# Rotary embedding in a decoder trunk: exchanging halves by ScalarE copies instead of permutation matmuls

## The chip, the cores and the metric

One core of one Trainium2 chip runs the kernel. The metric is the device time of one execution in microseconds (us), the median over several runs. TensorE multiplies matrices (PE in the profile, its weight loads PEld), VectorE is DVE, ScalarE is ACT, GpSimd is POOL, and SyncE (SP) issues most loads.

## What is computed

The reference is a trunk of two identical layers over 512 tokens of width 1024. A layer normalises x, projects it with one wide matrix, runs four causal mixers on the parts (forgetting attention "fox", gated linear attention "gla", retention "ret", and the state-space mixer "ssd"), gates and sums them, and adds a SwiGLU block. The change touches the rotary embedding of the retention mixer alone: q and k, four heads of 64 each, have their two halves of 32 turned against each other.

```
def apply_rotary(x, cos, sin):
    x1, x2 = xf[..., :half], xf[..., half:]        # half = 32 of a head's 64
    return concatenate([x1 * cos - x2 * sin, x1 * sin + x2 * cos])

o_c = retention_chunked(apply_rotary(heads(rq), cos, sin),
                        apply_rotary(heads(rk), cos, sin), heads(rv), log_gamma)
```

So an output element is its own value times cosine, plus or minus the value 32 rows away times sine.

## The kernel before, in words

Activations lie transposed: features on the 128 partitions, the 512 tokens along the row. A tile of q or k of the retention mixer is 128 x 512 and holds two heads, so the exchange of halves is an exchange between neighbouring groups of 32 partitions. There are two such tiles of q (`rq`) and two of k (`rk`) per layer.

Matrices are multiplied in float32r, a rounded float32, in two or three passes: an operand is split into a rounded part and a difference (`split`, line 211: a copy on ACT, a subtraction on DVE), and `mm3` (line 200) makes three matmuls of them, `mm2` (line 206) two, where one operand is an exact constant.

Weights come in pieces of eight 128 x 128 blocks. `load` (line 245) issues one transfer on SP into one of two buffers, and `convert` (line 257) splits it, so each piece costs one ACT cast (L212) and one DVE subtraction (L213) of 128 x 1024. The pool of pieces has three buffers of each kind (line 139). The order of the blocks is that in which the program asks for them.

A projection (`proj`, line 435) is 8 blocks times three matmuls of 512 columns into one PSUM bank of the pool `pm`, which has four (line 144). `scaled` (line 484) takes it out of the bank with one DVE product (L487 or L489) into a tile from the pool `tp`, which has 33 tiles of 128 x 512 (lines 174 and 176). Mixers' own products go into four other banks, the pool `px` (line 145).

The order of work is written by hand. Each mixer is a generator that yields between steps. `drain` (line 462) runs one and, at each yield, lets `pull` (line 455) take projections, gates and up-projections from the list `fill`, until their stated costs reach the yield's weight times the mixer's entry in `PACE` (line 41). The list is filled at lines 1182 to 1195. The projections of `rq` and `rk` are the last four of the twelve that are listed before `ssd()`, and so are pulled towards the end of that mixer (lines 1184 and 1185). After that come `gla()`, `ret()` and `fox()`. The program is then given to a planner with a simulated timeline (line 1503), which lays out the order on each engine and assigns the tiles' places.

`ret` (line 914) begins with the rotary embedding: `split_tile` of the four tiles (line 916), a yield of weight 0.8, the multiplication of each by the constant signed permutation `perm` (line 920), a yield, then for each tile the product of the permuted tile with `sinT` on DVE (line 925), the product of the tile itself with `cosT` on POOL (line 926), the sum on DVE (line 927), and a yield. Seven more yields follow in the rest of the mixer. `sinT` and `cosT` are made once per launch by `rotary` (line 352). The constants that must be exact are loaded and cast at the start by `constants` (line 313); `perm` is 128 of their 780 columns.

The lines that the diff leaves as they are but that its steps go through:

```
def drain(gen, us):
    for want in gen:
        pull(us * (1 if want is None else want))
...
fill += [keep(rq, j, C_RQ + P * j) for j in range(2)] + [keep(rk, j, C_RK + P * j) for j in range(2)]
drain(ssd(), PACE[0])
...
drain(gla(), PACE[1])
...
drain(ret(), PACE[2])
```

Of the kernel before, what the change touches and what calls it, by code (L numbers as in the profile page):

```python
# [13 lines left out]
AF = mybir.ActivationFunctionType  # L14
# [4 lines left out]
P = 128  # L19
# [18 lines left out]
WARM = 11  # L38
TILE = 5.2
LAG = 1  # L40
PACE = (4.5, 5.0, 5.0, 7.5)
WIDE = 256 + 28
PARTS = (6, 6, 6, 4)
PLAIN = 2
# [11 lines left out]
def _const_parts():  # L56
    i = np.arange(P)
    same = (i[:, None] // 64) == (i[None, :] // 64)
    up = (i[:, None] <= i[None, :]).astype(np.float64)
    perm = np.zeros((P, P))  # L60
    for m in range(P):
        if m % 64 < 32:
            perm[m + 32, m] = -1.0
        else:
            perm[m - 32, m] = 1.0
    dret = np.zeros((P, NH, P))
    rel = i[None, :] - i[:, None]
    for h in range(NH):
        dret[:, h, :] = np.where(rel >= 0, np.exp(np.maximum(rel, 0) * LOGG[h]), 0.0) * 0.125
    qdec = np.zeros((P, 2, P))  # L70
    for j in range(2):
        for half in range(2):
            qdec[64 * half:64 * half + 64, j, :] = np.exp((i + 1.0) * LOGG[2 * j + half])[None, :]
    kdec = np.exp((P - 1.0 - i)[:, None] * LOGG[None, :]) * 0.125
    inv = (10000.0 ** (-np.arange(32) / 32.0))[i % 32][:, None]
    sgn = np.repeat(np.array([-1.0] * 4 + [1.0] * 8)[None, :], P, 0)
    one = np.ones((P, 1))
    exact = [
        ("uo", np.concatenate([up, np.ones((P, P))], 1)),
        ("lst", (i[:, None] > i[None, :]).astype(np.float64)),  # L80
        ("bones", same.astype(np.float64)),
        ("ubd", up * same),
        ("perm", perm),
        ("sel8", ((i[:, None] % 8 == np.arange(8)[None]) & (i[:, None] < 64)).astype(np.float64)),
        ("sel4", ((i[:, None] % 4 == np.arange(4)[None]) & (i[:, None] % 32 < 16) & (i[:, None] < 64)).astype(np.float64)),
    ]
    return exact, [
        ("ident", np.eye(P)),
        ("dret", dret.reshape(P, -1)),
        ("qdec", qdec.reshape(P, -1)),  # L90
        ("kdec", kdec),
        ("inv", inv),
        ("sgn", sgn),
        ("blk8", (i[:, None] // 8 == np.arange(4)[None]).astype(np.float64)),
        ("blk4", (i[:, None] // 4 == np.arange(4)[None]).astype(np.float64)),
        ("eps", one * EPS),
        ("one", one),
        ("hpi", one * (math.pi / 2)),
    ]
# [33 lines left out]
def trunk(ctx: ExitStack, tc: tile.TileContext, keys, qkeys, xin, pos, wst, wsq, par, ext, cst, out):  # L133
# [200 lines left out]
    def R(n):  # L334
        o, w = EXACT_OFF[n]
        return cr[:, o:o + w]

    ident = C("ident")
    lst, bones, ubd, perm, uo = (R(n) for n in ("lst", "bones", "ubd", "perm", "uo"))
    sel8 = R("sel8").rearrange("p (g r) -> p r g", g=2)  # L340
    sel4 = R("sel4")
    U, ones = uo[:, :P], uo[:, P:2 * P]
# [9 lines left out]
    def rotary():  # L352
        ang = TT()
        V.tensor_copy(out=ang, in_=posi.pop())
        V.tensor_scalar(out=ang, in0=ang, scalar1=C("inv"), scalar2=None, op0=ALU.mult)
        n = TT()
        V.tensor_scalar(out=n, in0=ang, scalar1=1.0 / (2 * math.pi), scalar2=12582912.0, op0=ALU.mult, op1=ALU.add)
        V.tensor_scalar(out=n, in0=n, scalar1=-12582912.0, scalar2=None, op0=ALU.add)
        for c in _two_pi_parts():
            V.scalar_tensor_tensor(out=ang, in0=n, scalar=-c, in1=ang, op0=ALU.mult, op1=ALU.add)  # L360
        V.tensor_scalar(out=ang, in0=ang, scalar1=3.1415925, scalar2=-3.1415925, op0=ALU.min, op1=ALU.max)
        act(out=sinT, in_=ang, func=AF.Sin)
        act(out=n, in_=ang, func=AF.Abs)
        act(out=cosT, in_=n, func=AF.Sin, scale=-1.0, bias=hpi)

# [69 lines left out]
    def proj(name, l, c, src, nk):  # L435
        ps = MM()
        for k in range(nk):
            mm3(ps, block(name, l, k, c), src[k], k == 0, k == nk - 1)
        return ps

    def layer(l, n1, scope):
# [67 lines left out]
        def keep(dst, i, c, scale=None):  # L509
            def go():  # L510
                dst[i] = scaled(proj("w_in", l, c, n1, KD), scale)
            return TILE, go

        def tokmajor(dst, c, stacked=False):
# [397 lines left out]
        yc = [None] * 2  # L912

        def ret():
            pp = []
            sr = [split_tile(t) for t in rq + rk]
            yield 0.8
            for t in sr:
                ps = MX()
                mm2(ps, perm, t, True, True)  # L920
                pp.append(ps)
            yield
            for ps, t in zip(pp, rq + rk):
                u = TT()
                V.tensor_tensor(out=u, in0=ps, in1=sinT, op=ALU.mult)
                G.tensor_tensor(out=t, in0=t, in1=cosT, op=ALU.mult)
                V.tensor_tensor(out=t, in0=t, in1=u, op=ALU.add)
            yield
            qd = []
            for j in range(2):  # L930
                t = TT()
                G.tensor_tensor(out=chunked(t), in0=chunked(rq[j]), in1=qdec[:, j].unsqueeze(1).broadcast_to([P, NB, P]), op=ALU.mult)
                qd.append(t)
            ms = {}
            for j in range(2):
                pa = [MX(), MX()]
                for tb in range(NB):
                    ts = slice(tb * P, (tb + 1) * P)
                    for half in range(2):
                        hs = slice(64 * half, 64 * half + 64)  # L940
                        mm(pa[half][:, ts], rk[j][hs, ts], rq[j][hs, ts], True, True)
                for half, ps in enumerate(pa):
                    t = TT()
                    V.tensor_tensor(out=chunked(t), in0=chunked(ps), in1=dret[:, 2 * j + half].unsqueeze(1).broadcast_to([P, NB, P]), op=ALU.mult)
                    ms[j, half] = t
                yield
            kt = []
            for j in range(2):
                ps = MX()
                for tb in range(NB):  # L950
                    T.transpose(ps[:, tb * P:(tb + 1) * P], rk[j][:, tb * P:(tb + 1) * P], ident)
                t = TT()
                V.tensor_tensor(out=t.rearrange("p (c h n) -> p c h n", c=NB, h=2), in0=ps.rearrange("p (c h n) -> p c h n", c=NB, h=2), in1=kdec[:, 2 * j:2 * j + 2].unsqueeze(1).unsqueeze(3).broadcast_to([P, NB, 2, 64]), op=ALU.mult)
                kt.append(t)
            yield
            ps = MX()
            pv = ps[:, :384].rearrange("p (c j n) -> p c j n", c=3, j=2)
            for c in range(3):
                for j in range(2):
                    for half in range(2):  # L960
                        hd = 2 * j + half
                        mm(pv[64 * half:64 * half + 64, c, j], kt[j][:, c * P + 64 * half:c * P + 64 * half + 64], rv[0][:, c, hd * 64:(hd + 1) * 64], True, True)
            for c in range(3):
                for half in range(2):
                    hs = slice(64 * half, 64 * half + 64)
                    if c == 0:
                        V.tensor_copy(out=sbd[hs, 0, :, hs], in_=pv[hs, 0])
                    else:
                        for j in range(2):
                            V.scalar_tensor_tensor(out=sbd[hs, c, j, hs], in0=sbd[hs, c - 1, j, hs], scalar=float(np.exp(P * LOGG[2 * j + half])), in1=pv[hs, c, j], op0=ALU.mult, op1=ALU.add)  # L970
            yield
            pos_ = [MX(), MX()]
            for j, po in enumerate(pos_):
                for c in range(NB):
                    ts = slice(c * P, (c + 1) * P)
                    for half in range(2):
                        hd = 2 * j + half
                        mm(po[64 * half:64 * half + 64, ts], rv[0][:, c, hd * 64:(hd + 1) * 64], ms[j, half][:, ts], c == 0, False)
            for j, po in enumerate(pos_):
                for c in range(1, NB):  # L980
                    ts = slice(c * P, (c + 1) * P)
                    mm(po[:, ts], sbd[:, c - 1, j], qd[j][:, ts], False, c == NB - 1)
            yield
            yield from headnorm(pos_, PR("rn"), gates["r"][2:], yc)
# [196 lines left out]

        fill += [keep(gq, j, C_GQ + P * j, 0.125) for j in range(2)] + [keep(gk, j, C_GK + P * j) for j in range(2)]
        fill += silus([C_GR, C_GR + P, C_RG, C_RG + P])
        fill += [keep(rq, j, C_RQ + P * j) for j in range(2)] + [keep(rk, j, C_RK + P * j) for j in range(2)]
        drain(ssd(), PACE[0])
        fill += tokmajor(rv, C_RV)
        fill += gate_quad(3, 0) + mix(gate_quad(3, 1), up_of(3, 0))
# [341 lines left out]
```

## Time and profile before

| | us |
|---|---|
| median of 3 runs | 1717.92 |
| lowest and highest | 1717.42, 1718.14 |
| profiled execution, its own time | 1718.72 |
| span of that execution in the profile | 1717.0 |

The profile shows one execution. Its span runs from the first to the last instruction of the program; 1.72 us of the execution's own time lie around it. Times of rows are microseconds from the span's start. A line such as L198 is a line of the kernel; where a helper records the instruction (`mm`, `split`, `act`), the line is the helper's, and the tile names tell which step it is. In a tile pair such as `mx<-t,cr` the left side is what is written (`mx` is a bank of the mixers, `mm` one of the projections), the right side what is read (`t` is a tile of the pool `tp`, `cr` the exact constants, `cs` the others, `xh` and `xl` the split activations, `wh` and `wl` the split weights).

### The profile page before, as it was taken

What the parts mean: (1) busy time and instruction counts of PE and PEld (TensorE: products, weight loads), DVE (VectorE), ACT (ScalarE), POOL (GpSimd) and SP (SyncE); (2) the same over time, 40 slices, a digit from 0 to 9 for tenths busy, and PEclk for the clock granted to TensorE, in tenths of its full rate; (3) what the DMA queues carried; (4) which work ended last, traced back from release to release, by engine and by line L of the source; (5) the groups of instructions that cost most, each with busy time, mean ns of one, the idle gap of its engine ahead of it and who ended that gap; (6) DMA issues with size and microseconds to landing.
All of it is one profiled execution on the core that took longest, in us unless ns stands there. A gap on an engine that the chain in (4) does not pass through costs nothing.

```text
span 1717.0 us, 25146 instructions
## 1 busy us (share of the span) xinstructions
PE 1705.9 (99%) x10140; PEld 1484.7 (86%) x10140; DVE 1213.2 (71%) x1683; ACT 861.9 (50%) x1190; POOL 225.2 (13%) x227
## 2 busy tenths in 40 slices
PE   8999999999999999999999999999999999999998
PEld 7878888888888999998988788888888889999998
DVE  5867666768677677675777666767776677767666
ACT  5424543546447646464544254435553574655543
POOL 2032110022101010101010322200221010101010
PEclk9999999999999999999999999999999999999999
DMA  5322222222235657575333222222222365665653
GB/s 199 106 74 74 75 82 78 86 86 74 78 112 143 196 134 186 135 186 121 89 99 115 68 74 75 85 76 89 83 86 82 103 172 161 152 175 139 183 108 102
DMA packets 54693, 195.00 MB, mean 114 GB/s; under 512 B 6064, under 2 KB 6448, under 8 KB 54576
## 3 DMA queue, kind: packets, MB, share of 16 engines
q1 hardware_dynamic: 45072, 160.45, 29.2%
q0 software_dynamic: 8640, 31.46, 10.3%
q8 instruction: 79, 1.29, 0.3%
q10 hardware_dynamic: 864, 1.48, 0.2%
q14 instruction: 38, 0.31, 0.1%
HBM read 191.27 MB, written 2.10 MB: 113 GB/s over the span
## 4 chain that ended last, share of the span: by engine, by line
PE 97%; DVE 1%; DMA 1%; ACT 1%; issue 0%; ACTq 0%; DVEq 0%
PE mm L198 65%; PE mx L198 31%; PE mx L1079 0%; DMA x<-in_x_dram 0%; DMA t<-in_ext_dram 0%; ACT wh L212 0%; DVE wl L213 0%; PE mx L679 0%; DVE t L369 0%; ACT L231 0%; DVE t L836 0%; ACT g L236 0%; DVE t L1168 0%; DVE n L407 0%; PE mx L871 0%
## 5 line engine op out<-in xcount | busy, mean ns | idle before, releaser
L212 ACT CAST wh<-wr 128x1024 fp32r<-128x1024 f32 (+1 forms) x240 | 250.0, 1043 | 378.4 <-PE mm L198 238.0
L198 PE MATMUL mm<-xh,wh 128*128 128x512 f32 (+1 forms) x1184 | 429.2, 362 | 0.9 <-DVE t L1168 0.9
L198 PE MATMUL mm<-xh,wl 128*128 128x512 f32 (+1 forms) x1184 | 428.6, 362 | 0.0
L198 PE MATMUL mm<-xl,wh 128*128 128x512 f32 (+1 forms) x1184 | 427.4, 361 | 0.0
L213 DVE TENSOR_TENSOR wl<-wr,wh 128x1024 fp32r<-128x1024 f32 (+1 forms) x220 | 281.8, 1282 | 119.9 <-ACT wh L212 117.6
L198 PEld LDWEIGHTS mm<-xh,wh 128*128 128x128 f32 x1184 | 222.6, 188 | 35.2 <-DVE t L1168 1.8
L198 PEld LDWEIGHTS mm<-xh,wl 128*128 128x128 f32 x1184 | 222.6, 188 | 35.1 <-issue 1.5
L198 PEld LDWEIGHTS mm<-xl,wh 128*128 128x128 f32 x1184 | 222.6, 188 | 33.7 <-issue 1.1
L198 PE MATMUL mm<-t,wh 128*128 128x512 f32 x448 | 140.3, 392 | 0.0
L198 PE MATMUL mx<-xh,wh 128*128 128x256 f32 (+1 forms) x448 | 136.2, 311 | 3.0 <-ACT wh L212 3.0
L198 PE MATMUL mx<-xl,wh 128*128 128x256 f32 (+1 forms) x448 | 138.5, 309 | 0.0
L1287 POOL DMA_DIRECT2D wl<-in_wsq_dram x60 | 51.9, 864 | 518.0 <-ACT wl L1286 337.1
L198 PE MATMUL mx<-f,wh 128*128 128x512 f32 x352 | 108.3, 390 | 0.0
L198 PE MATMUL mm<-f,wh 128*128 128x512 f32 x352 | 106.0, 390 | 0.0
L198 PEld LDWEIGHTS mm<-t,wh 128*128 128x128 f32 x448 | 83.3, 188 | 17.1
L213 DVE TENSOR_TENSOR l<-rq,wh 128x1024 fp32r<-128x1024 f32 x60 | 73.2, 1219 | 33.1 <-ACT wh L212 18.7
L198 PEld LDWEIGHTS mx<-xh,wh 128*128 128x128 f32 x448 | 84.1, 188 | 9.2 <-ACT wh L212 4.0
L198 PE MATMUL mx<-xh,wl 128*128 128x256 f32 (+1 forms) x288 | 91.0, 327 | 0.0
L198 PEld LDWEIGHTS mx<-xl,wh 128*128 128x128 f32 x448 | 84.2, 188 | 5.1
L198 PE MATMUL mm<-t,wl 128*128 128x512 f32 x224 | 87.5, 390 | 0.0
L212 ACT CAST wh<-rq 128x1024 fp32r<-128x1024 f32 x60 | 62.9, 1049 | 43.9 <-PE mm L198 21.5
L198 PEld LDWEIGHTS mm<-f,wh 128*128 128x128 f32 x352 | 66.1, 188 | 13.5
(275 smaller groups left out, 3457.2 us busy)
## 6 DMA issues: line engine op xcount, KB each, us to landing
wr<-in_wst_dram SPq DMA_DIRECT2D x216, 512.0 KB, 3.5
rq<-in_wsq_dram SPq DMA_DIRECT2D x60, 512.0 KB, 5.3
wl<-in_wsq_dram POOLq DMA_DIRECT2D x60, 512.0 KB, 7.1
wr<-in_wsq_dram SPq DMA_DIRECT2D x20, 512.0 KB, 7.3
out_dram<-x SPq DMA_DIRECT2D x8, 256.0 KB, 2.0
x<-in_x_dram SPq DMA_DIRECT2D x3, 512.0 KB, 7.2
wr<-in_wst_dram SPq DMA_DIRECT2D x4, 256.0 KB, 5.6
x<-in_x_dram SPq DMA_DIRECT2D x2, 256.0 KB, 4.5
```

The costliest lines, as they stand in the source:

```text
L198: T.matmul(o, lhsT=l, rhs=r, start=start, stop=stop, skip_group_check=True)
L212: A.copy(out=hi, in_=src)
L213: V.tensor_tensor(out=lo, in0=src, in1=hi.bitcast(F32), op=ALU.subtract)
L1287: G.dma_start(out=lo, in_=wsq[j], accum_op=ALU.add)
```

## The change

The permutation matmuls, their splits and the constant go. In place of `keep`, the four tiles of `rq` and `rk` get a new entry of the list, `turned`, which does the whole rotary embedding right behind the evacuation of the projection: four ACT copies of 32 partitions each write the tile with its halves exchanged into a second tile, and then the two products and the sum are made as before, the product with `sinT` now reading that second tile where it read a PSUM bank. The sign of the permutation moves into `sinT`, as a scale of its one activation by a constant column `turn`. The three yields of the removed part go, and the pace of `ret` rises from 5.0 to 7.0.

```diff
-PACE = (4.5, 5.0, 5.0, 7.5)
+PACE = (4.5, 5.0, 7.0, 7.5)
...
-        ("perm", perm),
...
+        ("turn", np.where(i % 64 < 32, -1.0, 1.0)[:, None]),
...
-        act(out=sinT, in_=ang, func=AF.Sin)
+        act(out=sinT, in_=ang, func=AF.Sin, scale=C("turn"))
...
+        def turned(dst, i, c):
+            def go():
+                t = dst[i] = scaled(proj("w_in", l, c, n1, KD))
+                u = TT()
+                for a in range(0, P, 32):
+                    A.copy(out=u[a:a + 32], in_=t[a ^ 32:(a ^ 32) + 32])
+                V.tensor_tensor(out=u, in0=u, in1=sinT, op=ALU.mult)
+                G.tensor_tensor(out=t, in0=t, in1=cosT, op=ALU.mult)
+                V.tensor_tensor(out=t, in0=t, in1=u, op=ALU.add)
             return TILE, go
...
         def ret():
-            pp = []
-            sr = [split_tile(t) for t in rq + rk]
-            yield 0.8
-            for t in sr:
-                ps = MX()
-                mm2(ps, perm, t, True, True)
-                pp.append(ps)
-            yield
-            for ps, t in zip(pp, rq + rk):
-                u = TT()
-                V.tensor_tensor(out=u, in0=ps, in1=sinT, op=ALU.mult)
-                G.tensor_tensor(out=t, in0=t, in1=cosT, op=ALU.mult)
-                V.tensor_tensor(out=t, in0=t, in1=u, op=ALU.add)
-            yield
             qd = []
...
-        fill += [keep(rq, j, C_RQ + P * j) for j in range(2)] + [keep(rk, j, C_RK + P * j) for j in range(2)]
+        fill += [turned(rq, j, C_RQ + P * j) for j in range(2)] + [turned(rk, j, C_RK + P * j) for j in range(2)]
```

## Rows read from the trace of the kernel before

**Rows 1.** The page's first part, busy time of each engine with its share of the span and its instructions, and from its second part the granted clock of TensorE in 40 slices, in tenths of full speed.
```profile
PE 1705.9 (99%) x10140; PEld 1484.7 (86%) x10140; DVE 1213.2 (71%) x1683; ACT 861.9 (50%) x1190; POOL 225.2 (13%) x227
PEclk9999999999999999999999999999999999999999
```
**Rows 2.** All waits of PE over the whole span: who waited for whom, us in total, times, longest.
```profile
PE mx L198 <- ACT wh L212: 3.0, 3, 1.6
PE mm L198 <- POOL t L325: 1.4, 1, 1.4
PE mx L198 <- DVE t L213: 1.2, 2, 0.7
PE mm L198 <- DVE t L1168: 0.9, 2, 0.5
```
**Rows 3.** PE's timeline in layer 0: start, duration, engine, line, operation, tiles, shapes. Between the first two rows lie 27 more matmuls of projections, between the third and the fourth 18 more, six of them of the permutation (one row of the view can hold two).
```profile
244.72 0.39 PE L198 MATMUL mm<-xh,wh 128*128 128x512 f32 x1
...
251.07 0.40 PE L198 MATMUL mm<-xl,wh 128*128 128x512 f32 x1
251.30 0.40 PE L198 MATMUL mx<-t,cr 128*128 128x512 f32 x1
...
255.70 0.40 PE L198 MATMUL mx<-t,cr 128*128 128x512 f32 x1
255.94 0.39 PE L198 MATMUL mm<-xh,wl 128*128 128x512 f32 x1
```
**Rows 4.** PE's groups by line and shape: the group of all matmuls of 512 columns that read an exact constant, with their count, busy time, mean ns of one and idle time before them.
```profile
L198 PE MATMUL mx<-t,cr 128*128 128x512 f32 x96 | 35.0, 401 | 0.0
```
**Rows 5.** Two lines of the kernel by themselves: a cast of 32 partitions that stays in place (L610), and one of 64 partitions from one half to the other (L1045). Columns: count, duration in ns (min/median/max), first and last start, forms.
```profile
L610 ACT CAST t<-t x4: 618/620/622, 100.4 to 1143.4; 32x512 fp32r<-32x512 f32 x4
...
L1045 ACT CAST t<-t x8: 617/618/620, 341.8 to 1264.8; 64x512 fp32r<-64x512 f32 x8
```
**Rows 6.** The timeline of layer 0 at the retention mixer's split (L916, recorded at the lines of `split`): three ACT casts in a row, one DVE difference alone and three in a row, the idle time before them and who ended it in brackets.
```profile
247.62 1.66 ACT L212 CAST t<-t 128x512 fp32r<-128x512 f32 x3
...
246.79 0.69 DVE L213 TENSOR_TENSOR t<-t,t 128x512 fp32r<-128x512 f32 x1 [3.19 <-ACT t L212]
...
249.87 2.98 DVE L213 TENSOR_TENSOR t<-t,t 128x512 fp32r<-128x512 f32 x3
```
**Rows 7.** DVE's timeline in layer 0: evacuations of projections (L487). Where the idle time before one was ended by PE, it took the bank as soon as PE had filled it.
```profile
135.01 0.68 DVE L487 TENSOR_TENSOR t<-mm,n 128x512 f32<-128x512 f32 x1
...
146.77 1.28 DVE L487 TENSOR_TENSOR t<-mm,n 128x512 f32<-128x512 f32 x2
...
152.05 0.69 DVE L487 TENSOR_TENSOR t<-mm,n 128x512 f32<-128x512 f32 x1 [2.42 <-PE mm L198]
...
165.25 0.69 DVE L487 TENSOR_TENSOR t<-mm,n 128x512 f32<-128x512 f32 x1 [0.33 <-PE mm L198]
```
**Rows 8.** Busy time of each engine in three stretches of layer 0 (start:end, length, then PE, PEld, DVE, ACT and POOL with their instructions, granted clock, DMA share, GB/s).
```profile
146.00:166.00 20.00, 20.00 (x135) 15.98 (x134) 14.12 (x21) 13.32 (x20) 5.54 (x5) 1.00 0.23 78
166.00:186.00 20.00, 20.00 (x144) 18.74 (x143) 14.85 (x20) 13.21 (x25) 2.27 (x5) 1.00 0.25 79
...
247.00:262.00 15.00, 15.00 (x67) 12.38 (x66) 14.63 (x17) 4.38 (x6) 9.48 (x6) 1.00 0.19 70
```
**Rows 9.** The list of waits over all engines: ACT's weight casts.
```profile
ACT wh L212 <- PE mm L198: 259.5, 98, 7.5
```
**Rows 10.** Timelines of layer 0: the last differences of the split of the state-space mixer's result on DVE, and the first up-projection on PE, which reads that result.
```profile
174.68 1.29 DVE L213 TENSOR_TENSOR t<-t,t 128x512 fp32r<-128x512 f32 x2
...
216.44 0.71 PE L198 MATMUL mm<-t,wh 128*128 128x512 f32 x2
```
**Rows 11.** The three elementwise lines of the rotary embedding, with the columns of rows 5.
```profile
L925 DVE TENSOR_TENSOR t<-mx,sinT x8: 673/678/680, 255.0 to 1109.6; 128x512 f32<-128x512 f32 x8
...
L926 POOL TENSOR_TENSOR t<-t,cosT x8: 1293/1702/2284, 247.6 to 1104.8; 128x512 f32<-128x512 f32 x8
...
L927 DVE TENSOR_TENSOR t<-t,t x8: 679/862/999, 255.8 to 1111.6; 128x512 f32<-128x512 f32 x8
```
**Rows 12.** The start of the launch: the second transfer of the exact constants among the DMA issues (queue, count, KB, us to landing), three pieces of the chain that ended last (start, us, what), and one stretch of the busy times with the columns of rows 8.
```profile
t<-in_ext_dram ACTq DMA_DIRECT2D x1, 134.0 KB, 5.5
...
1.74 5.54 DMA t<-in_ext_dram
...
7.30 7.24 DMA x<-in_x_dram
...
20.52 4.64 PE mx L198 x19
...
5.00:10.00 5.00, 3.42 (x18) 2.81 (x18) 2.64 (x4) 4.96 (x8) 1.02 (x2) 1.00 1.03 394
```
**Rows 13.** PE's timeline in layer 0 around the retention mixer's scores: 32 small full-precision matmuls between projections.
```profile
262.74 0.39 PE L198 MATMUL mm<-xh,wl 128*128 128x512 f32 x1
263.06 2.06 PE L198 MATMUL mx<-t,t 64*128 64x128 f32 x32
265.04 0.50 PE L198 MATMUL mm<-xh,wh 128*128 128x512 f32 x1
265.38 0.39 PE L198 MATMUL mm<-xl,wh 128*128 128x512 f32 x1
```

More of the change, by code (lines that the diff above doesn't have):

```diff
@@ L59, in _const_parts @@
     up = (i[:, None] <= i[None, :]).astype(np.float64)
[L60 to L65, printed above, removed]
     dret = np.zeros((P, NH, P))
@@ L338, in trunk @@
     ident = C("ident")
-    lst, bones, ubd, perm, uo = (R(n) for n in ("lst", "bones", "ubd", "perm", "uo"))
+    lst, bones, ubd, uo = (R(n) for n in ("lst", "bones", "ubd", "uo"))
     sel8 = R("sel8").rearrange("p (g r) -> p r g", g=2)
@@ L511, in go @@
                 dst[i] = scaled(proj("w_in", l, c, n1, KD), scale)
+            return TILE, go
+        def turned(dst, i, c):
[7 more added lines that the diff above has]
+                V.tensor_tensor(out=t, in0=t, in1=u, op=ALU.add)
             return TILE, go
```

## Prediction

> **What bounds the kernel now.** I read the page's engine line first: TensorE (PE) is busy for 99% of the span, VectorE (DVE) 71%, ScalarE (ACT) 50%, GpSimd (POOL) 13%, and the granted clock is 9 tenths or more in every slice [rows 1]. Next the list of waits, for PE alone: 6.5 us in the whole span, 4.4 of them PE on ACT and POOL, and the other four waits, 2.1 us together, on DVE [rows 2]. So PE is the bound, and what is worth something is what PE's own stream loses.
>
> The busy time of a matmul is no price, since each overlaps the next; the distance between starts is. In a stretch without permutations PE makes 28 matmuls of 512 columns from 244.72 to 251.07, which is 6.35 / 28 = 0.2268 us each, and the rows read 0.39 us for the same thing [rows 3]. The even spacing shows that the 99% is real.
>
> **What PE loses.** In each layer the permutation is four products of two matmuls (L920), so eight of 512 columns, sixteen in all; they are among the 96 matmuls that read an exact constant with 512 columns [rows 4]. Between the starts at 251.07 and 255.94 PE runs 21 matmuls, these eight and 13 of a projection woven between them [rows 3]. It takes 4.87 us; 13 at 0.2268 are 2.95; the eight cost 1.92, 0.240 each. The weaving also shows that nobody waits for the permutation: the planner (line 1503) lays projections around it, and PE doesn't idle there. So its whole worth is its own time: 16 x 0.240 = 3.84 us. The lower bound is the plain spacing, 16 x 0.2268 = 3.63.
>
> The Trainium skill (TensorE: Matmul & The Clock Gate, "Wait — 56ns, not 53.3ns?") gives 215.7 ns between starts for 512 columns at the full clock; by that figure the term would be an estimated 3.45 us. The trace's own spacing is longer, and I use it.
>
> **What the split loses.** L916 makes a rounded copy on ACT (three take 1.66 us in a row; with 0.62 for the last one [rows 5] they are 0.52 apart) and a difference on DVE (0.69 alone, 2.98 for three beside POOL), four of each per layer [rows 6]. Per layer ACT loses 2.2 us and DVE 2.8 to 4.0. PE waits for neither there; worth 0, as nothing on the path is late by it.
>
> **What the copies add.** Each of the four tiles of a layer gets four copies of 32 partitions by 512. No row shows a copy between 32-partition groups. The nearest are a 32 x 512 cast that stays in place, 0.62 us, and a 64 x 512 cast from one half of the partitions to the other, 0.618 [rows 5]: fewer partitions are no cheaper, and crossing costs nothing. So 16 copies a layer take 16 x 0.52 = 8.3 us back to back, or 9.9 at the whole duration. I take 8.3, since the four follow each other on one tile. They come behind the evacuations of these projections (L487), the last four of which in layer 0 start between 146.77 and 165.25 [rows 7]. ACT is busy 13.32 us in 146 to 166 and 13.21 in 166 to 186, of 20 each [rows 8]: 26.5 + 8.3 = 34.8 of 40, with the upper price 36.4. They fit, but if all sixteen fell into the first 20 us they would need 21.6.
>
> What is queued behind them on ACT? First, weight casts (L212): these start when PE frees a piece, as 259.5 us of ACT's idle time ended so [rows 9]; there are three pieces (line 139), each worth 8 blocks of three matmuls, 24 x 0.2268 = 5.4 us of PE. Four copies ahead delay a cast by about 2.2 us, which the piece in hand covers. Second, the squares and norm of the SSD mixer, whose result PE first needs at 216.44, the first up-projection, while the last differences of its split on DVE end near 176 [rows 10]. Forty microseconds cover a delay of two to nine.
>
> **What moves.** The product with sinT (0.678 us, the same each time), the product with cosT on POOL (1.29 to 2.28) and the sum (0.68 to 1.00) keep their number [rows 11], and go from the retention stage to the SSD tail. The product with sinT will read two SBUF tiles in place of a PSUM bank and one; the nearest row of that kind is the sum, so 0.68 to 1.00. That adds at most 0.32 x 4 = 1.3 us per layer to DVE, which has 14.12 of 20 us busy there, while the stretch it leaves, 247 to 262, is almost full on DVE with 14.63 of 15 [rows 8]. The Trainium skill speaks against the move (SBUF — State Buffer, "Who interferes with whom"): a DVE instruction with two SBUF inputs and a POOL instruction that reads SBUF shut each other out for a whole instruction, so each product could wait for one cosT product. By that rule an estimated 8 x 1.29 us more waiting on DVE or POOL, none of it on PE. The constant 0.678 beside the spread of the sum agrees with the rule.
>
> DVE now waits for ACT's copies in its own queue, and behind it stand the evacuations of the next projections and the weight differences. This is priced as a rival below; as the forecast I take 0.
>
> **The pace.** The three yields that go were worth 0.8 + 1 + 1 of ten; 9.8 yields at 5.0 pull 49 us of projections into the retention stage, 7 at 7.0 pull 49. Equal, 0. The sign enters as a scale of the one sine activation that the whole launch makes, and its constant is one column: 0.
>
> **The head.** The table of exact constants is 128 columns narrower, 64 KB. The chain of waits begins with the second transfer of that table (134 KB, now 70), 5.54 us from 1.74; the load of x at 7.30 goes out only when it has landed, takes 7.24, and PE's unbroken run starts at 20.52 [rows 12]. From 5 to 10 us the engines move 394 GB/s [rows 12]; 64 KB is 0.16 us at that rate. Bounds: 0, if the next load is limited by the other traffic, and 0.5, three times its bytes, if the landing and the load behind it both move. I take 0.16.
>
> **Sum.** 3.84 + 0.16 = 4.00. The profiled execution took 1718.72 us, 1.72 over its span of 1717.0, and 0.80 above the median of 1717.92. So 1718.72 - 4.00 = 1714.72 by that execution, and 1713.9 as a median. With the bounds, 3.63 to 4.34: 1714.3 to 1713.6. A measurement of this kernel can tell about 0.2%, 3.44 us; the border is 1714.48, close above the forecast.
>
> **Rivals.**
> Order given back (1715.9). The planner lays out each engine's order, and one edit changes it elsewhere. Every visit of PE to small full-precision matmuls among the projections costs about 0.2 us: 0.32 from 262.74 to 263.06 in place of 0.227, and 0.34 from 265.04 to 265.38 [rows 13]. Ten more visits over two layers cost 2.0. For it: the SSD tail, where the work lands, is full of such visits. Against: as likely to be fewer.
>
> More gained (1711.8). PE waits four times on DVE, twice each for L1168 and L213 (0.9 + 1.2) [rows 2]; if DVE, relieved in the retention stage, runs ahead, these waits vanish: 2.1 more. Against: the work before them is much the same.
>
> Slower (1725). The working tiles come from a pool of 33 (line 174), and now each turned projection takes a second one. In the SSD stage evacuations already lag: none between 135.01 and 146.77, then two at once, while those at 152.05 and 165.25 wait for PE [rows 7]. So at 146.77 two of the four projection banks (line 144) are full and a third is filling. If every turned tile held the next back by its copies, POOL product and sum, 2.2 + 1.3 + 0.9 = 4.4 us, four make 17.6 per layer, against the 12 us or so by which an evacuation was late without a stall (135.01 to 146.77). PE would stall 5.6 us a layer, 11.2 in all: 1713.9 + 11.2. It decides from about 14 us of lag per layer; that is where the gain of 2 us a layer is gone. Against: the lag is over by 152, as the SSD's tiles are set free.
>
> Nothing comes off (1717.9): the planner leaves PE idle where the permutations were. Only if the retention stage had nothing else ready; 49 us of projections speak against it.
>
> **How the numbers follow.** Forecast 0.50, more gained 0.10, order given back 0.30, nothing 0.03, slower 0.07. Faster by over 0.2%: 0.50 + 0.10 = 0.60; within: 0.33; slower: 0.07. The range leaves out the slower case, nothing, and the outer half of more gained, and so goes from 1711.4 to 1717.2.
>
> **What would show it.** Right: 16 fewer matmuls that read exact constants with 512 columns (80), plain spacing unchanged at 0.227, PE's waits near 6.5 us, ACT over 16 us busy in the 20 us around the rotated projections, sixteen copies per layer near 0.62 us, the sinT product spreading up to 1.00. Wrong: new PE waits on DVE or ACT between 140 and 190, or in the same place of layer 1; a first up-projection later than 216 by more than a few microseconds; copies of over 1 us.

## The result, and the profile after

The changed kernel takes 1726.01 us (median of 6 runs, 1724.58 to 1726.90) against 1718.22 for the kernel before on the same chip (6 runs): a ratio of 1.0045, 95% interval 1.0035 to 1.0054. It is slower by 7.8 us. The prediction was 1713.9, with 1711.4 to 1717.2 as its range.

The profiled execution took 1726.06 us, with a span of 1724.3 where before it was 1717.0. From here on, lines of the changed kernel are those of its own file: `mm` is L192 (before L198), `split` L206 and L207 (L212 and L213), the up-projections' evacuation L1159 (L1168). The page's engine line, answering [rows 1]:

```profile
PE 1708.8 (99%) x10124; PEld 1485.1 (86%) x10124; DVE 1199.4 (70%) x1675; ACT 875.2 (51%) x1214; POOL 225.3 (13%) x227
```

PE makes 16 matmuls fewer and is busy 2.9 us longer. The 40 slices of the granted clock are all at 9 tenths or more, as before, and too coarse to show why. All waits of PE, answering [rows 2]:

```profile
PE mm L192 <- DVE t L1159: 6.7, 2, 3.3
PE mx L192 <- ACT wh L206: 2.7, 3, 1.2
PE mm L192 <- POOL t L319: 1.4, 1, 1.4
```

The first row is the one to read: the wait for the up-projections' evacuation, 0.45 us a layer before, is 3.34 us a layer now. PE's timeline at the two places, both at the start of the forgetting attention, some 75 us behind the place that the permutation matmuls had:

```profile
331.02 0.40 PE L192 MATMUL mx<-t,cr 128*128 128x512 f32 x1
334.76 0.80 PE L192 MATMUL mm<-xh,wh 128*128 128x512 f32 x1 [3.34 <-DVE t L1159]
335.35 0.63 PE L192 MATMUL mm<-xl,wh 128*128 128x512 f32 x1
335.78 0.63 PE L192 MATMUL mm<-xh,wl 128*128 128x512 f32 x1
...
337.86 0.40 PE L192 MATMUL mm<-xl,wh 128*128 128x512 f32 x1
...
1188.70 0.79 PE L192 MATMUL mm<-xh,wh 128*128 128x512 f32 x1 [3.34 <-DVE t L1159]
...
1194.41 0.45 PE L192 MATMUL mm<-xl,wh 128*128 128x512 f32 x1
```

Two losses stand here. The wait itself: 331.02 to 334.76 is 3.74 us for a step of 0.23. And what follows it: 335.35 to 335.78 is 0.43 us a matmul where it was 0.227 [rows 3]. Seven matmuls from 334.76 to 337.86 take 3.10 us, 1.5 more than at 0.227; in layer 1, 13 from 1188.70 to 1194.41 take 5.71, 2.8 more. The granted clock says so too, in the busy times of these stretches (start:end, length, then PE, PEld, DVE, ACT and POOL with their instructions, granted clock, DMA share, GB/s):

```profile
322.00:330.00 8.00, 8.00 (x36) 6.53 (x36) 4.99 (x7) 6.18 (x10) 0.00 (x0) 1.00 0.20 67
330.00:338.00 8.00, 4.66 (x15) 3.47 (x14) 7.53 (x12) 6.14 (x6) 0.00 (x0) 0.79 0.24 69
1184.00:1196.00 12.00, 8.66 (x26) 6.54 (x26) 11.52 (x18) 7.72 (x9) 0.00 (x0) 0.72 0.14 44
```

In 330 to 338 PE is busy for 4.66 of 8 us at a granted clock of 0.79; in the 8 us ahead of that the clock is 1.00. The matmuls at 0.43 us are at the lower of its two levels, 1.2 GHz.

Why the evacuation is late is on DVE, in the same stretch:

```profile
325.53 0.69 DVE L1159 TENSOR_TENSOR t<-mm,g 128x512 f32<-128x512 f32 x1
326.13 1.28 DVE L362 SCALAR_TENSOR_TENSOR t<-mx,t 128x512 f32<-128x512 f32 x2
328.95 0.69 DVE L362 SCALAR_TENSOR_TENSOR t<-mx,t 128x512 f32<-128x512 f32 x1 [1.55 <-ACT t L230]
330.47 1.23 DVE L207 TENSOR_TENSOR wl<-wr,wh 128x1024 fp32r<-128x1024 f32 x1 [0.83 <-ACT wh L206]
331.62 1.29 DVE L363 SCALAR_TENSOR_TENSOR t<-t,t 128x512 f32<-128x512 f32 x2
332.82 0.69 DVE L362 SCALAR_TENSOR_TENSOR t<-mx,t 128x512 f32<-128x512 f32 x1
333.42 0.69 DVE L363 SCALAR_TENSOR_TENSOR t<-t,t 128x512 f32<-128x512 f32 x1
334.02 1.28 DVE L1159 TENSOR_TENSOR t<-mm,g 128x512 f32<-128x512 f32 x2
```

L362 to L364 are the Newton steps of the forgetting attention's norm of q and k: a chain that waits for ACT's exponentials. One evacuation stands ahead of it, two behind eight more instructions, seven of the chain and a weight difference (L207). The same stretch of the kernel before, DVE (L368 to L370 are its Newton steps, L1168 the evacuation) and PE:

```profile
328.53 1.28 DVE L369 SCALAR_TENSOR_TENSOR t<-t,t 128x512 f32<-128x512 f32 x2
329.73 0.68 DVE L368 SCALAR_TENSOR_TENSOR t<-mx,t 128x512 f32<-128x512 f32 x1
330.33 1.28 DVE L1168 TENSOR_TENSOR t<-mm,g 128x512 f32<-128x512 f32 x2
```
```profile
330.22 0.40 PE L198 MATMUL mx<-t,cr 128*128 128x512 f32 x1
331.06 0.50 PE L198 MATMUL mm<-xh,wh 128*128 128x512 f32 x1 [0.45 <-DVE t L1168]
```

The two evacuations started at 330.33, behind six instructions of the chain (the weight difference was done ahead of it, at 323.24), and PE took the bank 0.45 us late. Now they start at 334.02, 3.7 us later, though PE comes to the place only 0.8 us later (331.02 against 330.22). Nothing in this stretch belongs to the rotary embedding. What differs is the order that the planner laid out.

The rest of what the change did: PE's group that answers [rows 4], the transfer that answers [rows 12], copies, sinT product and sum (columns of [rows 11]), and the two stretches of [rows 8].

```profile
L192 PE MATMUL mx<-t,cr 128*128 128x512 f32 x80 | 28.7, 402 | 0.0
```
```profile
t<-in_ext_dram ACTq DMA_DIRECT2D x1, 70.0 KB, 5.5
```
```profile
L513 ACT COPY t<-t x32: 614/617/622, 152.4 to 1025.3; 32x512 f32<-32x512 f32 x32
...
L514 DVE TENSOR_TENSOR t<-t,sinT x8: 691/692/1787, 155.0 to 1026.0; 128x512 f32<-128x512 f32 x8
...
L516 DVE TENSOR_TENSOR t<-t,t x8: 679/693/1782, 158.9 to 1028.0; 128x512 f32<-128x512 f32 x8
```
```profile
146.00:166.00 20.00, 20.00 (x137) 16.04 (x137) 15.44 (x19) 15.51 (x23) 9.49 (x6) 1.00 0.21 55
166.00:186.00 20.00, 20.00 (x133) 18.30 (x132) 16.91 (x24) 14.33 (x25) 4.12 (x3) 1.00 0.26 78
```

The matmuls are gone, the copies cost what the 32 x 512 cast cost [rows 5], and in the last two rows, the place where they now stand, PE is busy for 20.00 of 20 us at the full clock.

**The sum of 7.3 us of span.** Removed matmuls: -3.8. The wait, 6.7 in place of 0.9: +5.8. The clock: 1.5 and 2.8, +4.3. That is 6.3. Of the remaining 1.0, I can place +1.2 (matmuls of up to 128 columns in layer 0 take 44.4 us by the distance of their starts, where it was 43.2: the retention scores among them 1.6 more, of which more under "The second price", while a wait of 0.5 on L213 is gone) and -1.1 (a stretch near the end in which this one execution of before ran slower, shown at the third experiment); 0.9 stays unplaced.

### The profile page after: what moved, and what is told of

Its sections match the earlier page's. It is cut to its first block, busy times and chain, and to the rows that moved or that the text cites. A ratio compares the mean times of both kernels' runs of the same rounds, so it can differ in the third digit from the quotient of the medians.

```text
span 1724.3 us, 25119 instructions
## 1 busy us (share of the span) xinstructions
PE 1708.8 (99%) x10124; PEld 1485.1 (86%) x10124; DVE 1199.4 (70%) x1675; ACT 875.2 (51%) x1214; POOL 225.3 (13%) x227
## 4 chain that ended last, share of the span: by engine, by line
PE 97%; DVE 1%; DMA 1%; ACT 0%; issue 0%; SPq 0%; DVEq 0%
PE mm L192 66%; PE mx L192 31%; PE mx L1070 1%; DMA x<-in_x_dram 0%; DMA wr<-in_wst_dram 0%; DVE t L363 0%; PE mx L684 0%; DVE wl L207 0%; ACT wh L206 0%; DVE t L841 0%; PE mx L942 0%; PE mx L876 0%; DVE n L401 0%; DVE t L847 0%; DVE t L1159 0%
## 5 line engine op out<-in xcount | busy, mean ns | idle before, releaser
L206 ACT CAST wh<-wr 128x1024 fp32r<-128x1024 f32 (+1 forms) x240 | 250.0, 1043 | 393.8 <-PE mm L192 239.1
L192 PE MATMUL mm<-xh,wh 128*128 128x512 f32 (+1 forms) x1184 | 430.4, 363 | 6.7 <-DVE t L1159 6.7
L192 PE MATMUL mm<-xh,wl 128*128 128x512 f32 (+1 forms) x1184 | 429.9, 363 | 0.0
L192 PE MATMUL mm<-xl,wh 128*128 128x512 f32 (+1 forms) x1184 | 429.4, 363 | 0.0
L207 DVE TENSOR_TENSOR wl<-wr,wh 128x1024 fp32r<-128x1024 f32 (+1 forms) x220 | 275.5, 1254 | 141.7 <-ACT wh L206 139.1
L192 PEld LDWEIGHTS mm<-xh,wh 128*128 128x128 f32 x1184 | 223.5, 189 | 41.0 <-DVE t L1159 7.5
L192 PEld LDWEIGHTS mm<-xl,wh 128*128 128x128 f32 x1184 | 223.5, 189 | 34.9 <-issue 1.6
L192 PEld LDWEIGHTS mm<-xh,wl 128*128 128x128 f32 x1184 | 223.5, 189 | 34.4 <-issue 0.9
L192 PE MATMUL mm<-t,wh 128*128 128x512 f32 x448 | 140.7, 393 | 0.0
L192 PE MATMUL mx<-xh,wh 128*128 128x256 f32 (+1 forms) x448 | 135.9, 310 | 2.7 <-ACT wh L206 2.7
L192 PE MATMUL mx<-xl,wh 128*128 128x256 f32 (+1 forms) x448 | 138.3, 309 | 0.0
L192 PE MATMUL mx<-f,wh 128*128 128x512 f32 x352 | 108.2, 390 | 0.0
L192 PE MATMUL mm<-f,wh 128*128 128x512 f32 x352 | 105.9, 389 | 0.0
L192 PEld LDWEIGHTS mm<-t,wh 128*128 128x128 f32 x448 | 83.4, 188 | 17.3
L207 DVE TENSOR_TENSOR l<-rq,wh 128x1024 fp32r<-128x1024 f32 x60 | 73.2, 1221 | 32.7 <-ACT wh L206 18.6
L192 PEld LDWEIGHTS mx<-xh,wh 128*128 128x128 f32 x448 | 84.1, 188 | 8.8 <-ACT wh L206 3.8
L192 PE MATMUL mx<-xh,wl 128*128 128x256 f32 (+1 forms) x288 | 90.9, 327 | 0.0
L192 PEld LDWEIGHTS mx<-xl,wh 128*128 128x128 f32 x448 | 84.1, 188 | 5.1
L192 PE MATMUL mm<-t,wl 128*128 128x512 f32 x224 | 87.5, 391 | 0.0
L206 ACT CAST wh<-rq 128x1024 fp32r<-128x1024 f32 x60 | 63.0, 1050 | 43.7 <-PE mm L192 17.9
L192 PEld LDWEIGHTS mm<-f,wh 128*128 128x128 f32 x352 | 66.1, 188 | 13.5
```

The source lines that it names most:

```text
L192: T.matmul(o, lhsT=l, rhs=r, start=start, stop=stop, skip_group_check=True)
L206: A.copy(out=hi, in_=src)
L207: V.tensor_tensor(out=lo, in0=src, in1=hi.bitcast(F32), op=ALU.subtract)
```

## The experiments

Theory 1: not the copies but the edit of pace and yields costs, by where it puts the up-projections' evacuations. Theory 2: the rotary work in the state-space tail makes ACT and DVE late. Theory 3: the permutation matmuls were not worth 3.8 us.

**e1: the kernel after, with pace and yields undone.**

```diff
-PACE = (4.5, 5.0, 7.0, 7.5)
+PACE = (4.5, 5.0, 5.0, 7.5)
...
         def ret():
+            yield 0.8
+            yield
+            yield
             qd = []
```

> The kernel after with one part undone: the pace of the retention mixer back to 5.0 and its three yields (0.8, 1, 1) back at its start; the copies, the new place of the products and the missing permutation matmuls stay. Theory 1 (the edit of pace and yields moved the norm chain of the forgetting attention ahead of the up-projections' evacuations): no wait of PE over 1 us on L1159's evacuations, no fall of the granted clock, 1714 us (1713 to 1716). Theory 2 (the copies and products in the state-space tail make DVE and ACT late): 1722 to 1727, the two waits of 3.3 us still there. Theory 3 (the permutation matmuls were worth next to nothing): 1717 to 1719 without the waits.

Measured: 1715.44 us (11 runs), ratio to before 0.9984, interval 0.9975 to 0.9993. Copies, products and their place are those of the kernel after. Its page and PE's wait for the evacuation (here L1162):

```profile
PE 1703.6 (99%) x10124; PEld 1481.4 (86%) x10124; DVE 1206.6 (70%) x1675; ACT 876.7 (51%) x1214; POOL 228.1 (13%) x227
```
```profile
PE mm L192 <- DVE t L1162: 0.9, 2, 0.5
```

The wait is back at 0.9, and 10.6 us are back with it. Theory 2 has fallen.

**e2: the kernel before, with the new pace and without the three yields, and nothing else changed.**

```diff
-PACE = (4.5, 5.0, 5.0, 7.5)
+PACE = (4.5, 5.0, 7.0, 7.5)
...
-            yield 0.8
             for t in sr:
...
-            yield
             for ps, t in zip(pp, rq + rk):
...
-            yield
             qd = []
```

> The kernel before, permutation matmuls and their split kept in place, with nothing changed but the pace of the retention mixer (7.0) and its three first yields (removed). Theory 1: PE waits about 3 us in each layer at the start of the forgetting attention, the granted clock falls behind it, and the time is 1725 to 1729 (1718.2 + 7 of waits + 1 to 4 for the clock). Theory 2: as before, 1717 to 1719, since no copy stands in the state-space tail.

Measured: 1733.30 us (4 runs, 1730.58 to 1735.70), ratio 1.0092, interval 1.0076 to 1.0107. PE's longest waits, and the busy times at the forgetting attention of layer 0 and of layer 1:

```profile
PE mm L198 <- DVE t L1165: 6.7, 2, 3.3
PE mx L198 <- DVE t L925: 6.1, 2, 3.1
```
```profile
334.00:346.00 12.00, 8.66 (x31) 6.87 (x31) 11.94 (x21) 7.82 (x9) 0.00 (x0) 0.86 0.14 44
1190.00:1200.00 10.00, 6.66 (x30) 5.17 (x29) 8.86 (x14) 7.03 (x7) 0.00 (x0) 1.00 0.15 52
```

Without a single copy, the same 6.7 us of waiting for the same evacuation: the first row has the numbers of the first row of the kernel after. The time lies above what I expected, by a second wait that I had not seen coming: 6.1 us on L925, which in this kernel is the rotary sum. The three yields were also what put projections between the permutation and the scores that need its result: in layer 0, 7 matmuls of projections stand there now, where 31 stood before. The kernel after, whose rotary work is long done by then, does not need that cover.

**e3: the kernel before without permutation.** It leaves the exchange of halves out.

```diff
-            sr = [split_tile(t) for t in rq + rk]
...
-                mm2(ps, perm, t, True, True)
...
-                V.tensor_tensor(out=u, in0=ps, in1=sinT, op=ALU.mult)
+                V.tensor_tensor(out=u, in0=t, in1=sinT, op=ALU.mult)
```

> The kernel before with the permutation matmuls and their split left out and nothing in their place: the halves are not exchanged, and the product with sinT reads the tile itself; yields and pace as before. It measures the worth of the removed matmuls. Theory 1 and the prediction's term: 1718.2 - 3.8 = 1714.4 (1713.5 to 1715.5). Theory 3: 1717 to 1719.

Measured: 1715.55 us (11 runs), ratio 0.9985, interval 0.9977 to 0.9994, so 2.65 off the median (1718.2), not 3.84. In the profile PE is busy 3.7 us less than in [rows 1]. The page, and a stretch of the last block:

```profile
PE 1702.2 (99%) x10124; PEld 1480.0 (86%) x10124; DVE 1212.8 (71%) x1675; ACT 857.5 (50%) x1182; POOL 228.1 (13%) x227
```
```profile
1659.40:1669.40 10.00, 10.00 (x90) 10.00 (x90) 6.76 (x8) 5.63 (x9) 0.86 (x1) 1.00 0.60 108
```

But 1.1 of that is no gain of the edit. The stretch holds 90 matmuls in 10 us; the same work in the kernel before, at the same clock:

```profile
1662.00:1672.00 10.00, 10.00 (x84) 9.83 (x84) 6.14 (x8) 5.08 (x9) 0.86 (x1) 1.00 0.60 114
```

There it is 84, and in the 10 us behind it 87 against 91: this one execution of before made ten matmuls less in these 20 us, at 0.11 each, and e2, which has the permutation, gains the same 1.1 there. So 2.6 is left, in agreement with the runs. The matmuls that read exact constants, 80 in place of 96, do take 3.76 us less by the distance of their starts. But 1.5 come back in the matmuls of up to 128 columns (43.2 to 44.0 us in layer 0, 37.5 to 38.3 in layer 1), 1.3 of it in the scores of retention, where 0.7 is a new wait on the rotary sum (L921), 0.36 us twice. Theory 3 is half right: the matmuls cost what was said, and a third of it is not gained.

**e4: the kernel after, pace 7.0, with the evacuation ahead of the chain.**

```diff
-            for i, u in enumerate(rs_):
+            for u in rs_:
                 act(out=u, in_=u, func=AF.Exp, scale=-0.5)
+            yield 1
+            for i, u in enumerate(rs_):
                 newton(u, pn[i], 64)
...
-            yield 2
+            yield 1
```

The edit moves two things: the four exponentials now stand ahead of the whole chain, and one of the two units of the yield stands between them and the chain.

> The kernel after, pace 7.0, with one thing moved in the forgetting attention alone: the yield of weight 2 between its exponentials and its Newton chain is split into one of 1 behind the exponentials and one of 1 behind the chain, so that the evacuation of the first up-projection stands ahead of the chain on DVE. Theory 1: the waits of 3.3 us are gone or below 1 us, no fall of the clock, 1714 to 1717. Theory 2: the copies are where they were, so 1722 to 1727.

Measured: 1718.34 us (11 runs), ratio 1.0001, interval 0.9992 to 1.0010. DVE in the same stretch, the page, and PE's wait:

```profile
325.60 1.28 DVE L1161 TENSOR_TENSOR t<-mm,g 128x512 f32<-128x512 f32 x2
...
330.54 1.23 DVE L207 TENSOR_TENSOR wl<-wr,wh 128x1024 fp32r<-128x1024 f32 x1 [0.83 <-ACT wh L206]
...
333.49 0.68 DVE L1161 TENSOR_TENSOR t<-mm,g 128x512 f32<-128x512 f32 x1
```
```profile
PE 1705.7 (99%) x10124; PEld 1483.2 (86%) x10124; DVE 1205.3 (70%) x1675; ACT 874.7 (51%) x1214; POOL 224.9 (13%) x227
```
```profile
PE mm L192 <- DVE t L1161: 1.1, 2, 0.6
```
```profile
360.66 0.50 PE L192 MATMUL mm<-xh,wh 128*128 128x512 f32 x1 [0.56 <-DVE t L1161]
```

Two evacuations ahead of the chain in place of one, and PE no longer waits at this place: the 1.1 us that are left stand some 30 us further on, at 360.66 and its like in layer 1. The kernel is 7.7 us faster by it than the kernel after. The weight difference still stands in the chain at 330.54, as late as in the kernel after, and the next evacuation, inside the chain, comes at 333.49, only 0.5 us earlier than the late pair there. So neither the weight difference nor a quicker chain decides, but the place of the second evacuation.

But theory 1 wanted 1714 to 1717. The same 10124 matmuls at the same clock keep PE busy 2.1 us longer than in e1, and nothing in the list of waits says why. So the kernel with pace 7.0 and without the three yields has a second price.

**e5, e6, e8: the kernel after at pace 6.5, 8.0 and 7.5.** The number in `PACE` is the only edit.

> The kernel after with the pace of the retention mixer at 6.5 in place of 7.0, and nothing else changed (no yields put back). In its order the next projection behind the norm's constant matmuls needs its bank 8 matmuls later, and that bank's evacuation is the 12th DVE instruction of the chain, where in the kernel after it is the next matmul and the 14th instruction, with a weight difference among those ahead. Theory 1 (which instruction the up-projections' evacuations stand behind): no wait over 1 us, no fall of the clock, 1714 to 1718. Theory 2 (copies and products in the state-space tail): 1722 to 1727.

> The kernel after with the pace of the retention mixer at 8.0 in place of 7.0. In its order a projection begins 3 matmuls behind the norm's constant matmuls and needs a bank whose evacuation stands at the end of the norm chain on DVE. Theory 1: a wait of PE on DVE of 2 to 5 us in each layer at the forgetting attention again, 1721 to 1730. Theory 2: 1722 to 1727 with no such wait. If neither wait nor loss is there, theory 1's rule of which evacuation stands behind the chain is too simple.

> The kernel after with the pace of the retention mixer at 7.5 in place of 7.0. In its order no weight difference stands in the norm chain, and the first up-projection's evacuation is the 7th DVE instruction of the chain. Theory 1: waits of 0 to 1.5 us per layer, 1715 to 1721. Theory 2: 1722 to 1727.

Measured: 6.5 gives 1719.11 us (11 runs; ratio 1.0004, interval 0.9996 to 1.0013), 7.5 gives 1724.63 (4 runs; 1.0035, 1.0021 to 1.0048), 8.0 gives 1729.17 (4 runs; 1.0062, 1.0049 to 1.0076). PE's waits for the forgetting attention's casts (L206), at 6.5, 7.5 and 8.0:

```profile
PE mx L192 <- ACT t L206: 1.1, 2, 0.6
```
```profile
PE mx L192 <- ACT t L206: 3.5, 2, 1.7
```
```profile
PE mx L192 <- ACT t L206: 3.1, 2, 1.5
```

At 6.5 no wait of over 0.6 us there and no fall of the clock, as expected, yet 1.1 us above my bound: the second price again. At 8.0 the time is as expected, at 7.5 it is 3.6 above and would fit theory 2, if the waits were in the state-space tail. They are not, nor where I put them: the evacuation costs nothing at 7.5 and 0.4 us a layer at 8.0, and the longest wait stands further on, on a cast of the forgetting attention. Behind it the clock falls here too: it is 0.83 in the 10 us from 366 at 7.5, and in those from 398 at 8.0. My rule of which evacuation stands behind the chain reads one place of the order and doesn't name the next one.

**e7: the kernel before, with the copies in place of the permutation matmuls, pace and yields kept.**

```diff
-                mm2(ps, perm, t, True, True)
...
+                for a in range(0, P, 32):
+                    A.copy(out=u[a:a + 32], in_=t[a ^ 32:(a ^ 32) + 32])
-                V.tensor_tensor(out=u, in0=ps, in1=sinT, op=ALU.mult)
+                V.tensor_tensor(out=u, in0=u, in1=sinT, op=ALU.mult)
```

> The kernel before with the four-copy exchange in place of the permutation matmuls and their split, where they stood, at the start of the retention mixer (signed sine as in the kernel after); pace 5.0 and the three yields as before. Theory 1: the exchange by copies is worth the same wherever it stands, as long as pace and yields are kept: 1714.5 to 1716.5, with no wait over 1 us. Theory 2: the place of the copies decides; here none stands in the state-space tail, so 1714 to 1716 too, but then the kernel after with old pace and yields should not have reached 1715.4. A loss here (1717 to 1720) would say that the retention stage, where DVE is almost full, can't take the copies' wait.

Measured: 1722.45 us (11 runs), ratio 1.0025, interval 1.0016 to 1.0034: slower than before, and by more than the loss that I had named as the third case. PE and DVE at the retention mixer's start (L922 product, L923 POOL's product, L924 sum):

```profile
258.43 1.16 PE L199 MATMUL mx<-t,t 64*128 64x128 f32 x16 [2.51 <-DVE t L924]
```
```profile
251.37 0.69 DVE L922 TENSOR_TENSOR t<-t,sinT 128x512 f32<-128x512 f32 x1
253.25 1.76 DVE L924 TENSOR_TENSOR t<-t,t 128x512 f32<-128x512 f32 x1 [1.19 <-POOL t L923]
254.93 1.77 DVE L922 TENSOR_TENSOR t<-t,sinT 128x512 f32<-128x512 f32 x1
```

Here the copies are not free. The scores wait 2.5 us a layer for a rotary sum, since each tile is now copied (2.5 us on ACT), then multiplied and added on DVE at 1.57 to 1.77 us where it was 0.69, beside POOL's products. In the 10 us from 256 the granted clock is 0.83. So moving the exchange behind the projections is what makes it free. Theory 2 is turned round: the new place isn't the loss, the old place would be.

**e9: the kernel before, pace 5.5 in place of 5.0.** The number is the only edit.

> The kernel before, with the pace of the retention mixer at 5.5 in place of 5.0 and nothing else changed: permutation matmuls, split and yields stay, no copies. Its order at the forgetting attention is that of the kernel after with pace 8.0, which lost 6 us a layer from there to the SwiGLU block. Theory 1 (the pace by itself moves the time by such sums, whatever the rotary does): 1724 to 1732. Theory 2 (copies and products are what costs): 1717 to 1720.

Measured: 1736.32 us (4 runs), ratio 1.0104, interval 1.0090 to 1.0118: 18 us for a tenth more pace, with the rotary embedding as it was, and 4 us above the range that I gave. PE in layer 0, and the busy times there:

```profile
397.33 1.44 PE L198 MATMUL mx<-t,t 128*128 128x256 f32 x3 [5.42 <-DVE t L1044]
```
```profile
390.00:402.00 12.00, 6.58 (x24) 5.11 (x23) 7.83 (x12) 7.18 (x9) 2.91 (x3) 0.72 0.13 44
```

Another wait of PE on DVE in the forgetting attention (5.4 us on L1044, a difference of the stacked k), the same kind of fall of the clock behind it (0.72). The wait is not the one that the kernel after has at pace 8.0, though I had taken the two orders for equal.

**e10, e11: pace 5.0 with the yields at the end of the mixer (the diff is against the kernel after, beside the number), and e1 with e4's edit.**

```diff
             yield from headnorm(pos_, PR("rn"), gates["r"][2:], yc)
+            yield 0.8
+            yield
+            yield
```

> The kernel after with pace 5.0 and the three yields (0.8, 1, 1) at the end of the retention mixer, where the kernel of the first experiment has them at its start: the same 49 us of projections, 14 of them behind the mixer's steps in place of ahead of them. In its order the next projection after the norm's constant matmuls needs its bank 12 matmuls later (6 with the yields at the start). Theory 1: no wait on the up-projections' evacuation at all, 1714 to 1717. If it matters that projections stand ahead of the first retention step, PE waits there on DVE as in the kernel with copies in place (2.5 us a layer), and 1718 to 1722.

> The kernel of the first experiment (after, pace 5.0 and the yields back) with the split yield in the forgetting attention as well. The waits of 0.45 us on the up-projections' evacuation go: 1714.5, if nothing else moves; 1715 to 1718 if the other order costs visits of PE to small matmuls as it did with pace 7.0.

Measured: e10 1719.51 us (11 runs; ratio 1.0007, interval 0.9998 to 1.0016), e11 1715.23 (11 runs; 0.9984, 0.9975 to 0.9992). By their pages PE is busy 1706.9 and 1704.1 us with 10124 matmuls.

In e10 PE no longer waits for the evacuation, as expected, nor for the rotary sum, and it still lands 4 us above e1, in the second range that I gave but without its wait. In e11 the waits on the evacuation go from their place, but, other than I had expected, 1.1 us stand on it further on, as in e4, where e1 has 0.9. Its time can't be told from e1's; both beat the kernel before and the kernel after.

**The second price.** Counted in the trace's order, PE changes between small matmuls (up to 128 columns) and larger ones 219 times in e11, 223 in e1, 231 in e4, 235 in e10 and 239 in e5, at 1715.2, 1715.4, 1718.3, 1719.5 and 1719.1 us. Among these the time grows roughly with the changes, at 0.2 to 0.4 us each, more than the 0.1 (0.2 for a visit, in and out) that I read from [rows 13]. But e3 has 209 changes and takes 1715.6, no less than e1, so the count alone does not set the time. What the traces show is one kind of visit, to the retention scores, 32 matmuls on 64 partitions a layer. PE in e1, then in e4:

```profile
245.28 1.16 PE L192 MATMUL mx<-t,t 64*128 64x128 f32 x16
```
```profile
236.85 1.16 PE L192 MATMUL mx<-t,t 64*128 64x128 f32 x8
```

The visit of 16 takes 1.09 us from its first start to the next matmul's, and the matmuls in it start two at a time, 0.007 us apart. In the visit of 8 they start one by one, and it takes the same 1.09. Where the three yields stand ahead of the scores (e1, e11), each layer has two visits of 16, 4.4 us over both layers. Where they are gone (the kernel after, e4, e5, e6, e8), it has 8, 8 and 16, together 6.9 us at every pace from 6.5 to 8.0; with the yields at the end (e10) it has four of 8, together 8.7. Measured against e1, that is 2.5 of the 2.9 us that e4 loses, 2.5 of the 3.7 of e5, and 4.4 where e10 loses 4.1. So the second price goes with the missing yields ahead of the scores and not with the number in `PACE`. No run changes these visits alone, so that they are the cause is argued from the traces, not shown.

## Why the prediction was wrong

**The pace: here it failed.** The step was "9.8 yields at 5.0 pull 49 us of projections into the retention stage, 7 at 7.0 pull 49. Equal, 0." The sum is right and the 0 is not. e2 made this edit alone and lost 15.1 us; e1 took it alone out of the kernel after and won 10.6. Equal amounts in other lumps gave the planner another order 75 us later, at which I never looked: there the evacuation comes 3.7 us later, PE waits 6.7 us in place of 0.9, and the lower clock behind the waits costs 4.3. At the place itself the retention scores take 2.5 us more than with the yields (e1). The price of such a re-lay stood in the rival "order given back", as ten visits at 0.2, with no wait in it; the runs put it between 3 us (e4 against e1) and 18 us (e9).

**The permutation matmuls.** 16 x 0.240 = 3.84 us; by their starts 3.76, so the term was right as PE's own time. The step "PE doesn't idle there, so its whole worth is its own time" gave 1.2 too much: in e3, without these matmuls, the scores wait 0.36 us a layer, and the small matmuls take more. The runs say 2.65 (e3) and 2.76 (e1).

**The head.** 0.16 was predicted; the table lands in 5.5 us at 70 KB as it did at 134 KB. The lower bound, 0, was the right end.

**The copies.** Their duration was right (0.617 against 0.62), their spacing not: eight in a row on ACT take 5.04 us, 0.63 each, where I took 0.52 from casts. Even so their cost of 0 on PE stands: PE is busy for all of the 40 us around them in layer 0, and e1, with copies, takes 1715.44, where e3, with nothing in their place, takes 1715.55, 0.7 of it the scores' waits. ACT came to 15.51 of 20 us, not over 16.

**What moves.** I bounded the sinT product at 1.00 us; beside POOL it takes up to 1.79, and the sum 1.78. It cost PE nothing where the change put it, and together with the copies 2.5 us a layer where it was (e7). The rule that I cited and set at 0 (the Trainium skill, SBUF — State Buffer, "Who interferes with whom") agrees with these rows: a DVE instruction with two SBUF inputs waits for the POOL instruction that started ahead of it. The sinT product of 155.02 takes 1.77 us and ends 0.55 us behind POOL's product of 154.94, which takes 1.30; alone it takes 0.69. What this waiting does to PE was mine to place: at the old place such sums stand in a wait of PE (e7), at the new one PE stays busy.

**The rivals.** "Slower", 1725, hit the time by another road: its mechanism, tiles and evacuations late in the state-space tail, is not there, where PE is busy for all of 146 to 186. "Order given back", 1715.9, lies near what the rotary work did by itself (e1, 1715.4), where PE changes between small and larger matmuls 223 times in place of 213: five visits more, not ten. "More gained" had the waits for L1168 and L213 vanish; the second did, the first grew to 6.7.

**What would have shown it.** The list of signs was for the place where the work moved. No sign named the forgetting attention, though [rows 2] shows PE waiting 0.45 us twice on L1168: the bank was already late there.

## What to carry to other kernels

Where a planner or a hand-written pace lays out the order, an edit of that pace is priced by what it does to the tightest place downstream, not by whether its amounts add up; here one of the small waits that PE already had, 0.45 us, stood at the place where it later lost most. Try the edit of order and the edit of work in separate runs: here one was worth -2.8 us and the other +10.6. A wait of PE costs more than its length where the clock falls behind it.

## What was not expected of the hardware

The same wait of PE, 3.3 us, is followed by matmuls at the lower clock for 3.1 us in layer 0 of the kernel after, for 5.7 us in layer 1, and in layer 1 of e2 by none (granted clock 1.00 in 1190 to 1200 with 6.66 of 10 us busy). So the price of one and the same stall differed by up to 2.8 us, and e2's runs spread over 5 us where those of before spread over 3. What decides among these was not tried.

The retention scores were not expected either: matmuls on 64 partitions that start in pairs cost half of what they cost alone, 16 or 8 in the same 1.09 us, and an edit of the order can part the pairs.
